# Seven buffers for x by features, its rows behind the weights on one queue, and the value passes' last sum formed later

## The chip, the cores and the metric

The kernel runs on one core of a Trainium2 chip. The metric is the device time of one execution in microseconds; the kernel before has a median of 1997.19 us over three runs (1996.58 to 2002.1). Its five engines run side by side and meet at semaphores: PE (TensorE, matmuls; PEld is its weight load), DVE (VectorE), ACT (ScalarE), POOL (GpSimd) and SP, which here only issues transfers. DMAs are issued from SP's queue, a few from POOL's and ACT's.

## The reference

One decoder layer and a final norm over x of 512 tokens by 2048 features in float32 (names as in the reference, cut):

```
h = rmsnorm(x, ln_mix)                                # x: (512, 2048)
proj = h @ w_in                                       # w_in: (2048, 4608)
sb_q, sb_k, sb_v, sw_q, sw_k, sw_v = split(proj)      # 1024 1024 1024 | 1024 256 256
sb_o = stick_breaking_attention(sb_q, sb_k, sb_v)     # 16 heads of 64, causal
sw_o = sliding_window_sink_attention(sw_q, sw_k, sw_v, sinks, slopes)   # 16 heads, 4 kv heads
x = x + concat(rmsnorm(sb_o), rmsnorm(sw_o)) @ w_out
x = x + (silu(h2 @ w_gate) * (h2 @ w_up)) @ w_down    # h2 = rmsnorm(x, ln_ffn), width 5632
return rmsnorm(x, ln_final)
```

The change touches only the first part: half of `sw_q` (512 columns of `w_in`), then `sb_v` (1024 columns), and the sum of squares of x for the first norm.

## The kernel before

Every float32 operand of a matmul is split in two rounded parts, hi and lo, and a product is three matmuls (hi hi, lo hi, hi lo). ACT writes hi as a rounded copy, DVE writes lo as the difference. x comes in twice: by features (`x_cols`, tiles `xt` of 128 features by 512 tokens, from `load_cols`, usually two features' tiles in one transfer) and by rows (`xr`, 128 tokens by 2048, from `load_rows`). From each feature tile kt, 0 to 15, `h_make` makes `hhi` (ACT, line 255) and `hlo` (DVE, line 256) scaled by the norm's gain `gcol`; the row factor of the norm is applied after the products. The rows serve only `x_squares`: four ACT squares per row tile into `ss1`.

**The projection of the queries, `add_kq`.** The work is eight slabs of 256 rows of `w_in`, W0 to W7, 512 columns each. A slab is a transfer into `raw` (ring of three), a split into `whi` (ACT, line 203) and `wlo` (DVE, line 204; rings of two), and 24 matmuls of 512 columns into four banks, named m and o (lines 548 to 550). `split` of slab s+1 is called from `step` in the third of slab s's eight groups, and `load` of the next two. `prep` makes the feature tiles that a later slab needs (the list `KTS`), and a step after it runs `flush` (the sums waiting in `vsum`) and the squares of one row tile. Slab 0 is split in two halves (the `L117` rows on `raw`, 128x512).

**The value passes.** `sb_v` is formed in two passes g = 0 and 1 over 1024 features each, as a 2x2 block product with seven products instead of eight (order `PD`: 1, 7, 6, 4, 5, 2, 3), each in two halves: 28 slots, in `value_slot` and the loop after it. The left factors of products 5, 7, 6 and 3 are sums of blocks of x times gain: with a the first 256 tokens and b the last 256, unprimed for the pass's first four feature tiles and primed for its last four,

- s1 = b + b' (product 5), s3 = a - b (product 7), s2 = b' - s3 (product 6) and s4 = a' - s2 (product 3), written by `left_sums` in steps of 128x256 into tiles `vs`.

In the kernel before, POOL begins s1 from the rounded parts (`hhi` + `hlo`, half columns), and the flushes on DVE do the rest: one step per tile for the first four tiles of a pass (s3), three for the last four (s1, s2, s4). `form` splits a sum into `vf` (hi on ACT, lo on POOL). The right factors are weight differences that POOL forms (`difference`: `t` and in place in `raw`, 128x1024), split by ACT (`hp`, a hi in PSUM for DVE to subtract, and `whi`) and DVE (`wlo`). `take` adds a product's banks to the accumulators `vacc` and `vu` on DVE.

**What sets the order.** A scheduler orders each engine's instructions, except those that are kept in program order (`dma` on SP and the calls through `pV`, `pA`, `pG`, `pT`, all listed at line 117). An engine works its list strictly in order and so does a queue: an entry that waits holds all behind it. On SP's queue stand `xt`, all weights and the value weights; the row tiles are issued on POOL's queue. A buffer's next load waits for the last reader of what it held: a new `xt` for the flush that reads the old one, a new `raw` for its whi and wlo. The last part of the setup (calls at the end of `add_kq`'s part, from `add_kq()` to `load_rows`) writes out by hand in which order these loads are issued.

Of the kernel before, what the change touches and what calls it, by code (L numbers as in the profile page):

```python
# [37 lines left out]
def tile_hymba(ctx: ExitStack, tc: tile.TileContext, x, x_cols, gains, w_in, sinks, w_out, w_gu, w_dn, ln_fin, out):  # L38
# [96 lines left out]
    def constants():  # L135
        V.tensor_scalar(out=neg1, in0=ones, scalar1=-1.0, scalar2=None, op0=ALU.mult)
        scr = tmp(F32, "scr")[:, 0:P]
        G.affine_select(out=scr, in_=ones, pattern=[[-1, P]], compare_op=ALU.is_ge, fill=0.0,
                        base=0, channel_multiplier=1)
        V.tensor_scalar(out=negu, in0=scr, scalar1=-1.0, scalar2=None, op0=ALU.mult)  # L140
        scs = tmp(F32, "scs")[:, 0:P]
        G.affine_select(out=scs, in_=ones, pattern=[[-1, P]], compare_op=ALU.is_gt, fill=0.0,
# [20 lines left out]
    def load(i):  # L163
# [133 lines left out]
    def load_cols(kt, n):  # L297
        xt = phase[1].tile([P, n, 512], F32, tag="xt", name="xt", bufs=5)
        dma(out=xt, in_=x_cols[kt * P:(kt + n) * P, :].rearrange("(a p) s -> p a s", p=P))
        for k in range(n):  # L300
            xs[kt + k] = xt[:, k, :]

    def load_rows(t):
        xr.append(phase[1].tile([P, D], F32, tag="xr", name="xr", bufs=4))
        pG.dma_start(out=xr[t], in_=x2d[t * P:(t + 1) * P, :])

# [10 lines left out]
    def left_sums(kt, xt):  # L317
        g, j, gc = kt // 8, kt % 4, gcol[:, kt:kt + 1]
        if kt % 8 == 0:
            vs = [v8.tile([P, 4, 512], F32, tag="v8", name="vs") for _ in range(2)]  # L320
            for k, p in enumerate("5736"):
                vleft[g, p] = vs[k // 2][:, :, (k % 2) * 256:(k % 2) * 256 + 256]
        s1, s3, s4, s2 = (vleft[g, p][:, j, :] for p in "5736")
        a, b = xt[:, 0:256], xt[:, 256:512]
# [4 lines left out]
        if kt % 8 < 4:  # L329
            pG.tensor_tensor(out=s1, in0=f(h_hi[kt])[:, 256:512], in1=f(h_lo[kt])[:, 256:512], op=ALU.add)  # L330
            vsum.append(lambda: stt(s3, a, s1, ALU.subtract))
        else:
            vsum.append(lambda: (stt(s1, b, s1, ALU.add), stt(s2, b, s3, ALU.subtract), stt(s4, a, s2, ALU.subtract)))

# [242 lines left out]
    class ValuePass(Block):  # L577
# [38 lines left out]
        def form(self, p, part):  # L616
# [4 lines left out]
            else:  # L621
                hl = vfm[self.g, p]
                pG.tensor_tensor(out=hl[:, :, 256:512], in0=src, in1=f(hl)[:, :, 0:256], op=ALU.subtract)

    vp = [ValuePass(g) for g in range(2)]
    for g in range(2):
# [4 lines left out]
        for k, fn, *args in ((-4, u.sum, "7", 0), (-3, u.sum, "5", 0), (-2, u.form, "7", "l"), (-1, u.sum, "6", 0),  # L631
                             (0, u.sum, "7", 1), (1, u.sum, "5", 1), (2, u.form, "6", "l"), (3, u.sum, "6", 1),
                             (4, u.sum, "4", 0), (5, u.sum, "4", 1), (6, u.form, "5", "l"), (8, u.form, "3", "l")):
            at_slot(b0 + k, "sum", fn, *args)
        for k, p in ((-4, "7"), (0, "6"), (4, "5"), (7, "3")):
            at_slot(b0 + k, "late", u.form, p, "h")
        for k, p in enumerate(PD):
            at_slot(b0 + 2 * k + 2, "take", u.take, p)
# [1214 lines left out]
```

## Time and profile before

| what | us |
|---|---|
| median of three runs | 1997.19 (1996.58 to 2002.1) |
| the profiled execution, its own time | 1999.97 |
| its span, first to last instruction | 1998.2 |
| PE busy | 1971.4 |
| DVE, ACT busy | 1496.2, 1497.5 |
| POOL busy | 1005.0 |
| mean granted TensorE clock | 0.995 of full speed |

All numbers of the trace come from this one execution. Times in its rows count from the span's start. A timeline row gives start, length, engine, line, operation, output and input tiles (numbers left out) with partitions x elements, a count if instructions follow each other, and in brackets how long the engine sat idle before it and what ended that. A matmul's listed length is longer than the distance to the next, since matmuls are pipelined; the distance is what counts. A stage row gives the stage, its length, busy time (and count) of PE, PEld, DVE, ACT and POOL, the granted clock, the DMA engines' busy share and GB/s.

### The profile page before, as it was taken

What the parts mean: (1) busy time and instruction counts of PE and PEld (TensorE: products, weight loads), DVE (VectorE), ACT (ScalarE), POOL (GpSimd) and SP (SyncE); (2) the same over time, 40 slices, a digit from 0 to 9 for tenths busy, and PEclk for the clock granted to TensorE, in tenths of its full rate; (3) what the DMA queues carried; (4) which work ended last, traced back from release to release, by engine and by line L of the source; (5) the groups of instructions that cost most, each with busy time, mean ns of one, the idle gap of its engine ahead of it and who ended that gap; (6) DMA issues with size and microseconds to landing.
All of it is one profiled execution on the core that took longest, in us unless ns stands there. A gap on an engine that the chain in (4) does not pass through costs nothing.

```text
span 1998.2 us, 28817 instructions
## 1 busy us (share of the span) xinstructions
PE 1971.4 (99%) x10132; PEld 1677.1 (84%) x10132; DVE 1496.2 (75%) x2051; ACT 1497.5 (75%) x2007; POOL 1005.0 (50%) x445
## 2 busy tenths in 40 slices
PE   8899999999999999999999999999999999999998
PEld 6688888898888888888888888888888888888886
DVE  7666888888974787777777777777777867767767
ACT  6675878877762487777777777777777788788787
POOL 3660000000010067576666757666675778878883
PEclk9999999999999999999999999999999999999999
DMA  8224543522333445445344454535444734433423
GB/s 304 86 75 113 140 123 100 147 74 64 112 114 133 148 122 132 132 106 143 104 135 118 120 133 106 143 101 137 116 122 113 277 143 132 163 127 114 176 80 116
DMA packets 290912, 256.99 MB, mean 129 GB/s; under 512 B 12544, under 2 KB 233744, under 8 KB 287824
## 3 DMA queue, kind: packets, MB, share of 16 engines
q1 hardware_dynamic: 288384, 244.10, 41.4%
q0 software_dynamic: 1952, 9.71, 1.3%
q8 instruction: 80, 1.31, 0.3%
q10 hardware_dynamic: 432, 1.34, 0.2%
q14 instruction: 64, 0.52, 0.1%
HBM read 222.59 MB, written 19.92 MB: 121 GB/s over the span
## 4 chain that ended last, share of the span: by engine, by line
PE 94%; DVE 2%; ACT 2%; DMA 1%; issue 1%; SPq 0%; DVEq 0%; ACTq 0%
PE o L117 36%; PE m L117 30%; PE m L397 3%; PE m L398 3%; PE m L399 3%; PE m L361 2%; PE m L363 2%; PE m L362 2%; PE o L361 1%; PE o L363 1%; PE o L362 1%; PE z L911 1%; PE z L117 1%; PE o L939 1%; DVE vs L117 1%; DMA raw<-in_w_in_dram 1%
## 5 line engine op out<-in xcount | busy, mean ns | idle before, releaser
L117 DVE TENSOR_TENSOR wlo<-t,hp 128x1024 fp32r<-128x1024 f32 x247 | 301.1, 1219 | 184.6 <-PE o L117 114.0
L117 POOL TENSOR_TENSOR t<-raw,t 128x1024 f32<-128x1024 f32 x111 | 282.5, 2545 | 281.1 <-ACT hp L117 269.1
L117 ACT ACTIVATE whi<-t 128x1024 fp32r<-128x1024 f32 x247 | 262.1, 1061 | 127.4 <-PE o L117 77.3
L117 PE MATMUL o<-hca,whi 128*128 128x512 f32 x880 | 307.5, 394 | 0.0
L117 POOL TENSOR_TENSOR t<-raw,raw 128x1024 f32<-128x1024 f32 x114 | 295.1, 2592 | 24.6 <-issue 11.5
L117 DVE TENSOR_TENSOR wlo<-raw,hp 128x1024 fp32r<-128x1024 f32 x187 | 228.3, 1221 | 91.7 <-issue 52.1
L117 ACT ACTIVATE whi<-raw 128x1024 fp32r<-128x1024 f32 (+1 forms) x189 | 199.8, 1057 | 105.6 <-PE m L117 75.2
L117 ACT ACTIVATE hp<-t 128x1024 fp32r<-128x1024 f32 x247 | 249.2, 1009 | 1.9 <-POOL t L117 1.8
L117 PE MATMUL o<-hca,wlo 128*128 128x256 f32 x880 | 241.4, 277 | 0.0
L117 PEld LDWEIGHTS o<-hca,whi 128*128 128x128 f32 x880 | 164.7, 188 | 38.0
L117 ACT ACTIVATE hp<-raw 128x1024 fp32r<-128x1024 f32 x191 | 192.8, 1010 | 3.3 <-DMA raw<-in_w_down_dram 2.2
L117 PE MATMUL m<-hca,whi 128*128 128x512 f32 x528 | 186.1, 394 | 1.1 <-DVE hca L117 1.1
L117 PEld LDWEIGHTS o<-hca,wlo 128*128 128x128 f32 x880 | 164.5, 188 | 0.4
L204 DVE TENSOR_TENSOR wlo<-raw,whi 128x1024 fp32r<-128x1024 f32 x87 | 111.5, 1282 | 54.0 <-ACT whi L203 52.2
L203 ACT ACTIVATE whi<-raw 128x1024 fp32r<-128x1024 f32 x87 | 91.9, 1056 | 79.1 <-PE o L363 38.3
L709 POOL TENSOR_TENSOR sqA<-sqA,oc 128x512 f32<-128x512 f32 x7 | 10.0, 1432 | 274.5 <-ACT oc L708 274.5
L117 PE MATMUL m<-whi,dca 128*128 128x512 f32 x592 | 146.9, 389 | 0.0
L117 PE MATMUL o<-whi,dca 128*128 128x512 f32 x592 | 146.8, 389 | 0.0
L117 PE MATMUL m<-hca,wlo 128*128 128x256 f32 x528 | 144.8, 277 | 0.0
L117 PEld LDWEIGHTS o<-whi,dca 128*128 128x128 f32 x592 | 111.1, 188 | 23.1
L117 PEld LDWEIGHTS m<-whi,dca 128*128 128x128 f32 x592 | 111.1, 188 | 23.0
L117 PE MATMUL m<-hcs,whi 128*128 128x512 f32 x352 | 126.6, 394 | 0.0
(360 smaller groups left out, 5191.5 us busy)
## 6 DMA issues: line engine op xcount, KB each, us to landing
raw<-in_w_gate_up_dram SPq DMA_DIRECT2D x348, 256.0 KB, 5.1
raw<-in_w_down_dram SPq DMA_DIRECT2D x68, 512.0 KB, 5.2
raw<-in_w_in_dram SPq DMA_DIRECT2D x35, 512.0 KB, 4.6
raw<-in_w_in_dram SPq DMA_DIRECT2D x66, 256.0 KB, 3.5
raw<-in_w_out_dram SPq DMA_DIRECT2D x32, 512.0 KB, 3.7
aT<-w SPq DMA_DIRECT2D x44, 256.0 KB, 3.4
xd<-aT SPq DMA_DIRECT2D x10, 1024.0 KB, 6.8
rx<-in_w_down_dram SPq DMA_DIRECT2D x20, 512.0 KB, 5.7
```

What stands on the lines that cost most here:

```text
L117: return lambda *a, **k: tc.keep_in_program_order(fn(*a, **k))
L203: A.activation(out=hi, in_=raw, func=AF.Copy)
L204: V.tensor_tensor(out=lo, in0=raw, in1=f(hi), op=ALU.subtract)
L361: mm(o, lhsT=lh[:, sl], rhs=hi[:, j, :], start=first, stop=False, skip_group_check=halves)
L362: mm(o, lhsT=lh[:, sl], rhs=lo[:, j, :], start=False, stop=False, skip_group_check=halves)
L363: mm(o, lhsT=ll[:, sl], rhs=hi[:, j, :], start=False, stop=(k == nslab * a - 1), skip_group_check=halves)
L397: mm(o, lhsT=wh, rhs=xh, start=(k == 0), stop=False)
L398: mm(o, lhsT=wh, rhs=xl, start=False, stop=False)
L399: mm(o, lhsT=wl, rhs=xh, start=False, stop=(k == KT - 1))
L709: G.tensor_tensor(out=acc, in0=acc, in1=t, op=ALU.add)
L911: mm(zb[:, o:o + r.shape[1]], lhsT=lhsT, rhs=r, start=False, stop=last, skip_group_check=True)
L939: mm(H.ob[:, c0:S], lhsT=vb, rhs=r[:, o:o + S - c0], start=(k == 3 and r is B.h), stop=(k == 0 and r is B.l), skip_group_check=True)
```

## The change

Five edits, all before the attention.

1. `xt` has seven buffers instead of five, and `xr` three instead of four. The temporaries `scr` and `scs` of `constants` now lie in `maskf`.
2. The loads: within slab 0 each feature tile is issued ahead of its half of W0; after W2 come all remaining feature tiles, then W3 and row tile 0, W4 and row tile 1, W5 and 2, W6 and 3, all on SP's queue. Row tiles leave POOL's queue.
3. s1 is begun by ACT (`pA`, a scaled copy of b) instead of by POOL.
4. s4 leaves the flushes. `last_sum` forms it in two DVE steps of 128x1024 in slots 6 and 7 of each pass: the hi part of a' minus s2, then plus the lo part. Product 3's `form` moves back one slot.
5. `constants` is called in slot 14 instead of after eight steps.

```
-            pG.tensor_tensor(out=s1, in0=f(h_hi[kt])[:, 256:512], in1=f(h_lo[kt])[:, 256:512], op=ALU.add)
+            pA.activation(out=s1, in_=b, func=AF.Copy, scale=gc)
             vsum.append(lambda: stt(s3, a, s1, ALU.subtract))
         else:
-            vsum.append(lambda: (stt(s1, b, s1, ALU.add), stt(s2, b, s3, ALU.subtract), stt(s4, a, s2, ALU.subtract)))
+            vsum.append(lambda: (stt(s1, b, s1, ALU.add), stt(s2, b, s3, ALU.subtract)))
...
+        def last_sum(self, half):
+            s4 = vleft[self.g, "3"]
+            h = f(h8s[2 * self.g + 1][half])[:, :, 0:256]
+            if half:
+                pV.tensor_tensor(out=s4, in0=s4, in1=h, op=ALU.add)
+            else:
+                pV.tensor_tensor(out=s4, in0=h, in1=vleft[self.g, "6"], op=ALU.subtract)
...
-        for k, p in ((-4, "7"), (0, "6"), (4, "5"), (7, "3")):
+        for k, p in ((-4, "7"), (0, "6"), (4, "5"), (8, "3")):
             at_slot(b0 + k, "late", u.form, p, "h")
+        for k in range(2):
+            at_slot(b0 + 6 + k, "late", u.last_sum, k)
...
-        pG.dma_start(out=xr[t], in_=x2d[t * P:(t + 1) * P, :])
+        dma(out=xr[t], in_=x2d[t * P:(t + 1) * P, :])
...
-    load_cols(6, 2)
-    defer(8, constants)
-    for c in range(4, 8):
-        while pos[0] < c - 4 or pos[1] < 3:
+    for c in range(3, 8):
+        load_cols(2 * c, 2)
+    for c in range(4):
+        while pos[0] < c or pos[1] < 3:
             step()
-        load_cols(2 * c, 2)
-        load_rows(c - 4)
+        load(c + 3)
+        load_rows(c)
```

Past the value passes every engine's instructions stand in the same order as before. SP's queue at the start, before: one feature transfer (`xt`) and one slab's weights (`raw`) in turn after W2.

```order
L99 DMA xt<-in_x_cols_dram 128x2x512
L99 DMA raw<-in_w_in_dram 128x2x512
L99 DMA xt<-in_x_cols_dram 128x2x512 x2
L99 DMA raw<-in_w_in_dram 128x2x512
L99 DMA xt<-in_x_cols_dram 128x2x512
L99 DMA raw<-in_w_in_dram 128x2x512
L99 DMA xt<-in_x_cols_dram 128x2x512
L99 DMA raw<-in_w_in_dram 128x2x512
L99 DMA xt<-in_x_cols_dram 128x2x512
L99 DMA raw<-in_w_in_dram 128x2x512 x3
```

The rows are feature tiles 4 and 5, W2, 6 to 9, W3, 10 and 11, W4 and so on. The same place now, up to the first weights of the value pass (the second of the last two `raw`):

```order
L99 DMA xt<-in_x_cols_dram 128x2x512
L99 DMA raw<-in_w_in_dram 128x2x512
L99 DMA xt<-in_x_cols_dram 128x2x512 x5
L99 DMA raw<-in_w_in_dram 128x2x512
L99 DMA xr<-in_x_dram 128x2048
L99 DMA raw<-in_w_in_dram 128x2x512
L99 DMA xr<-in_x_dram 128x2048
L99 DMA raw<-in_w_in_dram 128x2x512
L99 DMA xr<-in_x_dram 128x2048
L99 DMA raw<-in_w_in_dram 128x2x512
L99 DMA xr<-in_x_dram 128x2048
L99 DMA raw<-in_w_in_dram 128x2x512 x2
```

All feature tiles stand ahead of W3 and the four row tiles between W3 and W7. ACT's list, which the first products wait for, from slab 1's whi to slab 4's, before:

```order
L203 ACTIVATE whi<-raw 128x1024
L255 ACTIVATE hhi<-xt,gcol 128x512 x2
L203 ACTIVATE whi<-raw 128x1024
L255 ACTIVATE hhi<-xt,gcol 128x512 x4
L203 ACTIVATE whi<-raw 128x1024
L117 ACTIVATE xr,ss_110<-xr 128x512 x4
L255 ACTIVATE hhi<-xt,gcol 128x512 x2
L203 ACTIVATE whi<-raw 128x1024
```

And now up to the first squares, with the sums begun on ACT (`vs`):

```order
L203 ACTIVATE whi<-raw 128x1024
L255 ACTIVATE hhi<-xt,gcol 128x512 x2
L203 ACTIVATE whi<-raw 128x1024
L255 ACTIVATE hhi<-xt,gcol 128x512 x4
L117 ACTIVATE vs<-xt,gcol 128x256 x2
L255 ACTIVATE hhi<-xt,gcol 128x512
L117 ACTIVATE vs<-xt,gcol 128x256
L255 ACTIVATE hhi<-xt,gcol 128x512
L117 ACTIVATE vs<-xt,gcol 128x256
L255 ACTIVATE hhi<-xt,gcol 128x512 x4
L203 ACTIVATE whi<-raw 128x1024
L117 ACTIVATE xr,ss_110<-xr 128x512 x4
```

Ten feature tiles and four sums stand ahead of W3's whi where four feature tiles stood. DVE's list from the last flush on, before, with `wlo` of W7 (line 204), the copies of the projection's banks (`kq`) and the first value weights:

```order
L204 TENSOR_TENSOR wlo<-raw,whi 128x1024
L117 SCALAR_TENSOR_TENSOR vs<-xt,gcol,vs 128x256 x6
L204 TENSOR_TENSOR wlo<-raw,whi 128x1024
L557 COPY kq<-m 128x512
L117 TENSOR_TENSOR wlo<-rx,hp 128x1024
L557 COPY kq<-o 128x512
```

And now, from the same place to the two steps of `last_sum` in the first pass (`vs<-hhi,vs` and `vs<-vs,hlo`):

```order
L204 TENSOR_TENSOR wlo<-raw,whi 128x1024
L117 SCALAR_TENSOR_TENSOR vs<-xt,gcol,vs 128x256 x4
L204 TENSOR_TENSOR wlo<-raw,whi 128x1024
L557 COPY kq<-m 128x512
L557 COPY kq<-o 128x512
...
L117 COPY vu<-m 128x512 x2
L117 TENSOR_TENSOR vs<-hhi,vs 128x4x256
L117 TENSOR_TENSOR wlo<-raw_415,hp 128x1024
L117 TENSOR_TENSOR vs<-vs,hlo 128x4x256
L117 TENSOR_TENSOR wlo<-raw_455,hp 128x1024
L117 COPY vacc<-o 128x512 x2
```

The last flush has four steps instead of six, and two steps on whole tiles stand between the value pass's copies and weight splits.

More of the change, by code (lines that the diff above doesn't have):

```diff
@@ L136, in constants @@
         V.tensor_scalar(out=neg1, in0=ones, scalar1=-1.0, scalar2=None, op0=ALU.mult)
-        scr = tmp(F32, "scr")[:, 0:P]
+        scr, scs = maskf[:, 0:P], maskf[:, P:2 * P]
         G.affine_select(out=scr, in_=ones, pattern=[[-1, P]], compare_op=ALU.is_ge, fill=0.0,
@@ L140, in constants @@
         V.tensor_scalar(out=negu, in0=scr, scalar1=-1.0, scalar2=None, op0=ALU.mult)
-        scs = tmp(F32, "scs")[:, 0:P]
         G.affine_select(out=scs, in_=ones, pattern=[[-1, P]], compare_op=ALU.is_gt, fill=0.0,
@@ L180, in load @@
             for j in range(a):
+                load_cols(j, 1)
                 dma(out=raw[:, j, :], in_=srcs[0][j * P:(j + 1) * P, :])
@@ L297, in load_cols @@
     def load_cols(kt, n):
-        xt = phase[1].tile([P, n, 512], F32, tag="xt", name="xt", bufs=5)
+        xt = phase[1].tile([P, n, 512], F32, tag="xt", name="xt", bufs=7)
         dma(out=xt, in_=x_cols[kt * P:(kt + n) * P, :].rearrange("(a p) s -> p a s", p=P))
@@ L303, in load_rows @@
     def load_rows(t):
-        xr.append(phase[1].tile([P, D], F32, tag="xr", name="xr", bufs=4))
-        pG.dma_start(out=xr[t], in_=x2d[t * P:(t + 1) * P, :])
+        xr.append(phase[1].tile([P, D], F32, tag="xr", name="xr", bufs=3))
+        dma(out=xr[t], in_=x2d[t * P:(t + 1) * P, :])
     def h_make(kt):
@@ L322, in left_sums @@
                 vleft[g, p] = vs[k // 2][:, :, (k % 2) * 256:(k % 2) * 256 + 256]
-        s1, s3, s4, s2 = (vleft[g, p][:, j, :] for p in "5736")
+        s1, s3, s2 = (vleft[g, p][:, j, :] for p in "576")
         a, b = xt[:, 0:256], xt[:, 256:512]
@@ L632, in tile_hymba @@
                              (0, u.sum, "7", 1), (1, u.sum, "5", 1), (2, u.form, "6", "l"), (3, u.sum, "6", 1),
-                             (4, u.sum, "4", 0), (5, u.sum, "4", 1), (6, u.form, "5", "l"), (8, u.form, "3", "l")):
+                             (4, u.sum, "4", 0), (5, u.sum, "4", 1), (6, u.form, "5", "l"), (9, u.form, "3", "l")):
             at_slot(b0 + k, "sum", fn, *args)
-        for k, p in ((-4, "7"), (0, "6"), (4, "5"), (7, "3")):
+        for k, p in ((-4, "7"), (0, "6"), (4, "5"), (8, "3")):
             at_slot(b0 + k, "late", u.form, p, "h")
+        for k in range(2):
+            at_slot(b0 + 6 + k, "late", u.last_sum, k)
         for k, p in enumerate(PD):
@@ L655, in tile_hymba @@
     add_kq()
-    load_cols(0, 1)
     load(0)
-    load_cols(1, 1)
     load_cols(2, 2)
@@ L768, in tile_hymba @@
             split(8)
+        if n == 14:
+            constants()
         vof(n, "product")
```

## The prediction

> **What bounds the kernel now.** I read the page, then busy time by stages, then TensorE's timeline where a stage has a hole, then what each hole waited for.
>
> ```profile
> PE 1971.4 (99%) x10132; PEld 1677.1 (84%) x10132; DVE 1496.2 (75%) x2051; ACT 1497.5 (75%) x2007; POOL 1005.0 (50%) x445
> ...
> 5.35:23.72 18.37, 17.49 (x75) 13.23 (x73) 14.01 (x24) 7.38 (x10) 8.55 (x13) 1.00 0.84 314
> 23.72:28.46 4.74, 0.16 (x1) 0.00 (x1) 0.02 (x1) 2.44 (x4) 0.00 (x0) 1.00 1.02 397
> 28.46:36.36 7.90, 7.38 (x19) 5.50 (x19) 7.90 (x12) 7.90 (x21) 2.97 (x3) 0.57 0.81 296
> ...
> 54.70:62.96 8.26, 0.00 (x1) 0.00 (x1) 8.17 (x3) 0.00 (x0) 7.04 (x3) 0.81 0.25 69
> 62.96:69.80 6.84, 6.84 (x23) 5.49 (x23) 2.51 (x3) 2.46 (x3) 0.00 (x0) 0.73 0.45 149
> 69.80:150.00 80.20, 80.20 (x355) 66.44 (x354) 53.32 (x64) 61.56 (x65) 51.82 (x26) 1.00 0.23 73
> 150.00:1990.00 1840.00, 1836.89 (x9567) 1567.44 (x9566) 1388.36 (x1916) 1399.47 (x1874) 923.71 (x388) 1.00 0.43 126
> ```
>
> The first number after a stage's length is PE busy; the last three are granted clock, DMA share, GB/s. From 69.80 to 1990 PE is busy 1917.1 of 1920.2 us: nothing there is to be had by feeding it better. Before 69.80, where the key and query projection runs, it sits idle twice and twice runs at a reduced clock.
>
> ```profile
> 5.35 0.48 PE L548 MATMUL m<-hhi,whi 128*128 128x512 f32 x1
> ...
> 13.60 0.72 PE L550 MATMUL m<-hhi,wlo 128*128 128x512 f32 x2 [0.77 <-DVE wlo L204]
> ...
> 18.28 0.39 PE L548 MATMUL m<-hhi,whi 128*128 128x512 f32 x1
> ...
> 23.49 0.39 PE L550 MATMUL o<-hhi,wlo 128*128 128x512 f32 x1
> 28.46 0.50 PE L548 MATMUL m<-hhi,whi 128*128 128x512 f32 x1 [4.58 <-ACT whi L203]
> ...
> 62.96 0.79 PE L550 MATMUL m<-hhi,wlo 128*128 128x512 f32 x1 [8.29 <-DVE wlo L204]
> ...
> 69.80 1.07 PE L117 MATMUL m<-whi,hhi 128*128 128x512 f32 x4
> ```
>
> 18.28 and 23.49 are the first and last of slab 2's 24 matmuls, 23 steps apart: 0.2265 us each, 5.44 a slab. Eight slabs need 43.5 us; from 5.35 to 69.80 they take 64.45. So 20.95 us is lost: 2.06 in slabs 0 to 2 (18.37 - 72 x 0.2265), 4.74 and 8.3 idle, about 3.4 and 1.85 to the clock (0.43 of 7.90, 0.27 of 6.84), and 0.6 in short waits. That is the ceiling.
>
> The first hole waits for slab 3's weights (W3). The queue's timeline, the chain, and two stages of the DMA:
>
> ```profile
> 4.81 10.05 SPq L99 DMA_DIRECT2D xt<-in_x_cols_dram  x2
> 14.96 0.41 SPq L99 DMA_DIRECT2D raw<-in_w_in_dram  x1
> ...
> 14.96 12.29 DMA raw<-in_w_in_dram
> ...
> 4.00:12.50 8.50, 8.38 (x37) 6.40 (x36) 5.10 (x9) 6.11 (x9) 4.84 (x8) 1.00 0.95 355
> 16.00:32.00 16.00, 10.89 (x42) 8.31 (x41) 9.62 (x17) 5.98 (x14) 0.97 (x2) 0.91 1.01 393
> ```
>
> The sixth transfer of x by features (xt) has no buffer until 14.9, W3 stands behind it, and it then shares a full DMA with x by rows (xr) from POOL's queue: 12.29 us to land. The second hole waits for wlo of W7:
>
> ```profile
> 46.56 13.07 DVE L117 SCALAR_TENSOR_TENSOR vs<-xt,gcol,vs 128x256 f32<-128x256 f32 x6
> 59.55 3.35 DVE L204 TENSOR_TENSOR wlo<-raw,whi 128x1024 fp32r<-128x1024 f32 x1
> ...
> 49.37 2.48 POOL L117 TENSOR_TENSOR raw<-raw,rx 128x1024 f32<-128x1024 f32 x1
> ...
> 59.42 2.40 POOL L117 TENSOR_TENSOR raw<-raw,rx 128x1024 f32<-128x1024 f32 x1
> ...
> 15.81 1.40 DVE L256 SCALAR_TENSOR_TENSOR hlo<-xt,gcol,hhi 128x512 fp32r<-128x512 f32 x2
> 17.14 1.21 DVE L204 TENSOR_TENSOR wlo<-raw,whi 128x1024 fp32r<-128x1024 f32 x1
> 18.27 0.87 DVE L117 SCALAR_TENSOR_TENSOR vs<-xt,gcol,vs 128x256 f32<-128x256 f32 x2
> ```
>
> Two vs take 0.87 us alone and six 13.07 beside POOL's weight differences, one per POOL instruction: DVE gets in only between them. wlo of W7 stands behind these six.
>
> **The change part by part.** Wn are the eight slabs' weights; each xt is 0.52 MB (the first two half), each W 0.52, each xr 1.05.
>
> *Seven xt buffers, W3 behind all xt.* The first xt to need an old buffer is now 12-13, at the first vs flush, not 8-9. What the step needs from ACT, in its timeline and groups:
>
> ```profile
> 8.53 1.34 ACT L255 ACTIVATE hhi<-xt,gcol 128x512 fp32r<-128x512 f32 x2
> 9.88 1.06 ACT L203 ACTIVATE whi<-raw 128x1024 fp32r<-128x1024 f32 x1
> ...
> 13.85 1.34 ACT L255 ACTIVATE hhi<-xt,gcol 128x512 fp32r<-128x512 f32 x2 [0.15 <-DMA xt<-in_x_cols_dram]
> ...
> 67.26 0.60 ACT L555 ACTIVATE kq<-m 128x512 f32<-128x512 f32 x1 [15.74 <-PE m L550]
> ...
> L117 ACT ACTIVATE xr<-xr 128x512 f32<-128x512 f32 x16 | 9.8, 614 | 0.0
> ```
>
> xt 0-7 and W0-W2, 3.67 MB, had landed by 13.8 (the row at 13.85 waits for the last of them). In the new order 2.62 MB more carry xt 8-15 and W3: at 393 to 355 GB/s W3 lands at 20.5 to 21.2 instead of 27.25, if the queue never runs dry: xt 8-11 (1.05 MB) keep it fed 2.7 us past 13.8, and the flush frees a buffer at about 12.9 (below). Each pair xr, W after it takes 4.0 to 4.4: W4 lands at 25, W5 29, W6 33, W7 37 to 39. Their slabs start at 29.0, 34.5, 39.9, 45.3 (below), less 2.3 for the split (1.06 on ACT, 1.21 on DVE): they are in time, and none of the 4.74 idle is left but what the next step adds.
>
> *First sum on ACT.* Eight 128x256 activations go onto ACT, four ahead of whi of W1, four among the hhi ahead of whi of W3. The trace has none; 128x512 costs 0.614 and 128x1024 1.06, so 256 columns cost 0.22 and I take 0.614 - 0.22 = 0.39, between 0.2 and 0.614. The first stands ahead of slab 0's whi: PE starts 0.4 later, at 5.75. By ACT's order whi of W1 ends at 11.2 (before 10.94) and wlo of W1 at 12.4, ahead of its first use; slab 1 starts at about 11.5, where 5.35 + 5.44 = 10.8 would be without loss. So the 0.77 wait goes and 0.7 of the 2.06 stays; slab 2 ends at 11.5 + 10.9 = 22.4. From 13.8 ACT has ten hhi (half of 1.34 each) and four sums, 8.3: whi of W3 starts at 22.1 and ends at 23.2, slab 3 waits 0.8. DVE, after wlo of W1, has four vs (0.39, what the second adds in the row at 18.27), two hlo (0.66), wlo of W2 until 16.5, four vs and nine hlo, 7.5, and wlo of W3 until 25.2, wanted after slab 3's seventh matmul at 24.8: 0.4. I take 1.2 in all, between 0 and 2.5 (sums at 0.614, DVE steps at half of 1.40 and 0.87). The wait of 0.77 left the clock of its stage at 1.00, so I charge none to these, and the 3.4 goes.
>
> *Row transfers on SP.* Four issues leave POOL's queue for SP's, each ahead of a W; behind xr3, which waits for the first squares, stand W7 and the value weights. The squares (four of 0.614 per slab) stand on ACT ahead of each whi from W4 on. xr0 lands at 23.4, its squares end at 25.9, xr3 lands at 36 to 38. ACT needs 2.5 + 1.06 of a slab's 5.44 and hides them: cost 0. Without that slack a late xr would go to PE one for one.
>
> *The flushes lose the last sum.* Eight 128x256 steps go from DVE, eight sums from POOL. The last flush (four vs, 1.6) runs behind wlo of W6, whose buffer slab 4 frees at 34.5: 34.5 + 1.06 + 1.21 = 36.7 to 38.3. POOL's first difference reads a tile that lands two transfers behind W7, 39 to 42. So the flush is past, and only wlo of W7 (from 41) can meet POOL: 2.5 and 1.2, done by 45, wanted at 45.8. All 10.1 of the second hole and its clock goes; between 0 and the second rival's price.
>
> *End of the projection.* 11.5 + 7 x 5.44 + 1.2 = 50.8 against 69.80. ACT now has the kq copy ahead of the first hp: 0.60 + 1.06 + 1.06 fill the 2.7 us after the matmuls it waits for. I charge 0.3, up to 1: 51.1.
>
> *The last sum in the value pass.* Two 128x1024 DVE steps on SBUF per pass, 1.21 each by the row at 17.14; the value pass on DVE and POOL:
>
> ```profile
> 87.53 1.28 DVE L117 COPY vu<-m 128x512 f32<-128x512 f32 x2
> 89.11 1.22 DVE L117 TENSOR_TENSOR wlo<-raw,hp 128x1024 fp32r<-128x1024 f32 x1 [0.30 <-PE o L117]
> 91.83 1.22 DVE L117 TENSOR_TENSOR wlo<-raw,hp 128x1024 fp32r<-128x1024 f32 x1 [1.50 <-PE o L117]
> ...
> 84.68 2.41 POOL L117 TENSOR_TENSOR vf<-vs,vf 128x1024 fp32r<-128x1024 f32 x1
> 91.22 2.40 POOL L117 TENSOR_TENSOR vf<-vs,vf 128x1024 fp32r<-128x1024 f32 x1 [4.13 <-ACT vf L117]
> ...
> 126.97 2.41 POOL L117 TENSOR_TENSOR vacc<-vacc,vu 128x1024 f32<-128x1024 f32 x1 [1.80 <-DVE vu L117]
> ```
>
> They stand behind the vu copies (88.8), one on each side of a wlo. DVE has 1.5 + 0.3 idle per two products, and a wlo is wanted 4.5 us after its buffer is free (20 matmuls), so 2.4 fits. In the first pass POOL is idle from 87.1 until the vf that now waits for this sum; in the second the accumulation at 126.97 starts at the same moment: one wait of 2.4, some 0.5 on PE. I take 0.5 in all, between 0 and the rival's 4.7.
>
> *The constants* are called later, but their instructions stand in the same place on DVE and POOL: 0.
>
> Sum: 0.7 + 1.2 + 0.3 + 0.5 = 2.7 stays, and 0.25 for short waits: 20.95 - 2.95 = 18.0. The profiled execution took 1999.97 (span 1998.2) and would take 1982.0; it lies 2.8 above the median of 1997.19, so the median goes to 1979.2.
>
> **The rivals.** *The first hole stays* (0.14): whi and wlo of W3 now stand behind all hhi and hlo, and behind xt 12-15, which wait for a flush. If that chain is 4 us late, PE idles as at 23.72 and the clock falls again: 4.7 + 3.4 stay, gain 11, 1986. For: ACT and DVE are full there; against: margins worked out above. The Trainium skill (TensorE: Matmul & The Clock Gate, "What's actually happening") says that about 3.4 us idle halves the clock and as much work restores it. By that the slow stretch would cost 1.7; here it lasted 7.9 us at 0.57.
>
> *The second hole stays* (0.07): POOL's weights come before the flush. Then four vs at 2.5 end at 46.7 and wlo of W7 at 50.4, wanted at 45.8: 4.6 and the clock's 3.4 stay, gain 10, 1987. Against: the tile is issued after vs that stand before it, and lands behind W7.
>
> *DVE is locked in the value passes* (0.07): each of the four steps, and DVE behind it, waits for a whole POOL instruction as at 46.56. Two such steps (2.4 + 1.2) and two wlo end 9.6 us after the products' start, wanted at 7.25 (32 matmuls): 2.35 on PE per pass, 4.7 in both, 4.2 more than charged: 1983. POOL's idle time from 87.1 speaks against. The Trainium skill (SBUF — State Buffer, "Who interferes with whom") states this lock: a VectorE instruction with two SBUF inputs and a GpSimd one that reads SBUF exclude each other for a whole instruction. The row at 46.56 agrees, and so does the wlo at 91.83, whose second input lies in PSUM: it takes its 1.22 beside POOL's vf at 91.22.
>
> *One queue is slower than two* (0.04): if xr and W on SP went one at a time, by the page's
>
> ```profile
> raw<-in_w_in_dram SPq DMA_DIRECT2D x35, 512.0 KB, 4.6
> ...
> xr<-in_x_dram POOLq DMA_DIRECT2D x4, 1024.0 KB, 8.0
> ```
>
> each pair would take 12.6, W7 land at 20.6 + 50.4 = 71, the projection end at 79: 9 later than now, 2006. It decides once W7 lands after 62, under 207 GB/s. Against: 355 GB/s from SP alone at 4.00.
>
> *Nothing measurable* (0.05): losses only move; 1997.
>
> **How the numbers follow.** My forecast has 0.63. With the rivals that stay faster, faster by over 0.3% (6 us, about what a measurement of this kernel can tell) has 0.91, the same 0.05, slower 0.04. The range: low 1975.0, all 20.95 gone and 1.2 for the spread of the runs; high 1987.0, which takes in the unknown costs, the lock and the first rival.
>
> **What would show it.** Right: no PE gap over 2 us between 5.7 and 52; W3 landing near 21; value products from about 51; the last flush under 2 us; clock 1.00 throughout. Wrong: a stage at 0.5 clock, W7 landing after 44, vs in the value passes over 2 us each with PE waiting for wlo.

## The result, and the profile after

The changed kernel takes 1984.44 us (median of four runs, 1983.54 to 1986.93) where the kernel before took 1997.51 in the same comparison (four runs, 1996.58 to 2002.1): ratio 0.9932, 95% interval 0.9914 to 0.995. That is 13.1 us between the medians, 0.68% by the ratio. The forecast was 1979.2 within 1975.0 to 1987.0, so the sign and the range were right and the gain of 18 was 5 too large.

The profiled execution took 1986.93, the slowest of its four. First the page's engine row, then stages of it (columns as before: stage, length, busy us and count of PE, PEld, DVE, ACT, POOL, granted clock, DMA share, GB/s):

```profile
PE 1970.0 (99%) x10132; PEld 1681.1 (85%) x10132; DVE 1484.3 (75%) x2047; ACT 1501.0 (76%) x2015; POOL 994.0 (50%) x433
```

```profile
5.00:6.00 1.00, 0.56 (x4) 0.33 (x4) 0.84 (x2) 1.00 (x3) 0.00 (x0) 1.00 0.60 96
6.00:7.00 1.00, 1.00 (x6) 0.82 (x5) 1.00 (x2) 0.61 (x2) 0.00 (x0) 1.00 0.53 117
...
12.00:14.40 2.40, 2.40 (x8) 1.81 (x7) 1.82 (x5) 2.40 (x5) 0.68 (x2) 0.50 1.05 387
14.40:54.06 39.66, 38.98 (x171) 31.75 (x170) 27.53 (x46) 28.31 (x59) 12.18 (x6) 1.00 0.88 339
54.06:150.00 95.94, 95.91 (x426) 79.10 (x426) 70.21 (x84) 72.22 (x82) 55.75 (x28) 1.00 0.25 78
...
800.00:1400.00 600.00, 600.00 (x3446) 527.30 (x3445) 434.76 (x493) 474.27 (x524) 387.13 (x154) 1.00 0.46 122
```

Behind 14.40 PE is as good as never idle: both holes are gone. But there is a stage at half clock that was not forecast (12.00 to 14.40), and ahead of it two microseconds in which the DMA moved 96 and 117 GB/s. The kernel before in the same microseconds, and in the long stretch:

```profile
5.00:6.00 1.00, 1.00 (x7) 0.86 (x6) 1.00 (x2) 0.19 (x1) 0.46 (x1) 1.00 0.99 354
6.00:7.00 1.00, 1.00 (x6) 0.75 (x5) 0.06 (x1) 0.00 (x0) 0.66 (x1) 1.00 1.00 365
...
800.00:1400.00 600.00, 600.00 (x3456) 524.41 (x3455) 435.21 (x493) 474.96 (x525) 389.23 (x155) 1.00 0.46 123
```

PE's timeline of the changed kernel, where it waits and at the first value product:

```profile
5.65 0.50 PE L548 MATMUL m<-hhi,whi 128*128 128x512 f32 x1 [0.44 <-ACT whi L117]
...
8.28 0.39 PE L550 MATMUL o<-hhi,wlo 128*128 128x512 f32 x1
10.26 0.50 PE L548 MATMUL m<-hhi,whi 128*128 128x512 f32 x1 [1.59 <-ACT whi L117]
...
28.29 0.73 PE L550 MATMUL m<-hhi,wlo 128*128 128x512 f32 x2 [0.68 <-DVE wlo L204]
...
54.06 1.20 PE L117 MATMUL m<-whi,hhi 128*128 128x512 f32 x4
```

The wait at 10.26, in the middle of slab 0, is new. ACT's row says what it is: the second half of W0 arrives late. And POOL's rows show what else was issued early, the transfer of the attention's `sink` constant, and that the last flush on DVE now ends ahead of POOL's first weight difference:

```profile
9.57 0.63 ACT L117 ACTIVATE whi<-raw 128x512 fp32r<-128x512 f32 x1 [2.96 <-DMA raw<-in_w_in_dram]
```

```profile
2.00 0.72 POOL L148 DMA_DIRECT2D sink<-in_swa_sinks_dram  x1
...
41.84 2.40 POOL L117 TENSOR_TENSOR t<-raw,raw 128x1024 f32<-128x1024 f32 x1 [27.40 <-DMA rx<-in_w_in_dram]
```

```profile
39.92 1.67 DVE L117 SCALAR_TENSOR_TENSOR vs<-xt,gcol,vs 128x256 f32<-128x256 f32 x4
...
73.14 1.21 DVE L117 TENSOR_TENSOR vs<-hhi,vs 128x1024 f32<-128x1024 f32 x1
...
75.39 1.22 DVE L117 TENSOR_TENSOR vs<-vs,hlo 128x1024 f32<-128x1024 f32 x1
...
111.22 1.22 DVE L117 TENSOR_TENSOR vs<-hhi,vs 128x1024 f32<-128x1024 f32 x1
...
113.48 2.31 DVE L117 TENSOR_TENSOR vs<-vs,hlo 128x1024 f32<-128x1024 f32 x1
```

The flush ends at 41.59, a quarter of a microsecond ahead of 41.84. That order is not chance. With seven `xt` buffers the tile `t`, which POOL's first difference writes, lies where the last feature transfer lay; the last reader of that is the last step of the flush, and the program has POOL wait for it. In the kernel before `t` lies where a row tile lay, and POOL waits for transfers alone. Three of the four steps of `last_sum` take the 1.21 that was charged; the one that meets POOL takes 2.31.

Where the 13.04 of the two profiled executions (1999.97 and 1986.93) come from: the first value product is 15.74 earlier (69.80, now 54.06); from there to the end it took 2.54 more (1928.40, now 1930.94), though PE has 0.03 idle in the 95.94 us after it; and the time outside the span grew by 0.16. So two things had to be explained: the late start, and a long stretch that is slower with PE busy all the time (3446 matmuls between 800 and 1400 us instead of 3456).

### The profile page after: what moved, and what is told of

Its sections match the earlier page's. It is cut to its first block, busy times and chain, and to the rows that moved or that the text cites. A ratio compares the mean times of both kernels' runs of the same rounds, so it can differ in the third digit from the quotient of the medians.

```text
span 1985.0 us, 28804 instructions
## 1 busy us (share of the span) xinstructions
PE 1970.0 (99%) x10132; PEld 1681.1 (85%) x10132; DVE 1484.3 (75%) x2047; ACT 1501.0 (76%) x2015; POOL 994.0 (50%) x433
## 4 chain that ended last, share of the span: by engine, by line
PE 95%; ACT 2%; DVE 1%; DMA 0%; issue 0%; SPq 0%; DVEq 0%; ACTq 0%
PE o L117 36%; PE m L117 30%; PE m L397 3%; PE m L398 3%; PE m L399 3%; PE m L361 2%; PE m L363 2%; PE m L362 2%; PE o L361 1%; PE o L363 1%; PE o L362 1%; PE z L921 1%; PE z L117 1%; PE o L949 1%; PE z L1120 1%; PE z L874 1%
```

## The experiments

Every kernel was compared with the kernel before on the same chip. The first column of times is the first value product in its profile, which sums up the part that the change touches. Where two variants are compared below, their medians are. The four from "the same again" to "last sum only" share one chip, the next four a second, the next three a third; as 3456 and 3445 matmuls come on the first of these, and 3456 and 3408 on the second, that count does not go by the chip.

| kernel | first value product | matmuls 800 to 1400 | median us (runs) | ratio to before, 95% interval |
|---|---|---|---|---|
| before (first profile) | 69.80 | 3456 | 1997.51 (1996.58 to 2002.1) | |
| changed kernel | 54.06 | 3446 | 1984.44 (1983.54 to 1986.93) | 0.9932 [0.9914, 0.995] |
| the same again | 53.99 | 3456 | 1984.23 (1983.67 to 1984.49) | 0.9933 [0.9916, 0.9951] |
| late sink | 51.27 | 3456 | 1981.07 (1980.82 to 1981.54) | 0.9918 [0.9901, 0.9935] |
| loads only | 53.24 | 3445 | 1984.48 (1983.7 to 1986.27) | 0.9936 [0.9915, 0.9958] |
| last sum only | 60.52 | 3456 | 1989.29 (1988.47 to 1991.38) | 0.9964 [0.9949, 0.9979] |
| late sink, first sum on POOL | 52.01 | 3457 | 1982.59 (1982.37 to 1982.82) | 0.9917 [0.9902, 0.9931] |
| late sink, s4 in the flushes | 50.59 | 3457 | 1981.13 (1980.94 to 1981.36) | 0.9909 [0.9894, 0.9924] |
| late sink, W3 ahead | 49.99 | 3456 | 1980.24 (1979.93 to 1980.78) | 0.9905 [0.9888, 0.9923] |
| POOL gated | 59.06 | 3408 | 2001.25 (2000.47 to 2001.68) | 1.0013 [1.0003, 1.0022] |
| POOL gated in place | 59.02 | 3445 | 1991.4 (1989.45 to 1992.59) | 0.9984 [0.9968, 1.0001] |
| W3 ahead, 128 bytes on | 49.75 | 3409 | 1991.06 (1990.58 to 1991.46) | 0.9978 [0.9961, 0.9996] |
| W3 ahead, 96 bytes on | 50.03 | 3425 | 1987.14 (1986.45 to 1987.37) | 0.9954 [0.9938, 0.9969] |
| before again | 70.17 | 3456 | 2000.62 (one run) | |

**The changed kernel again.** No edit.

> The changed kernel unaltered, to see whether its late start repeats. In its first profile the second half of W0 landed near 9.5 us, PE waited 1.59 us for it, and PE ran at a reduced clock to 14.4. Theory A (the sink's transfer, issued on POOL's queue at 2.00 us, holds up SP's transfers): the same again, DMA under 150 GB/s between 5 and 7 us, a wait of 1.2 to 2.0 us in slab 0. Rival B (chance of that one execution): the half lands near 7, no wait, the first value product near 51. Time 1983.5 to 1987 by A, 1981 by B. The long stretch behind 54 us took 2.5 us more in that execution than before; if this is a property of the execution and not of the change, it may be gone here (first value product to the end 1928.4 instead of 1930.9).

The late start repeats, with 85 and 148 GB/s between 5 and 7 us; the slower stretch does not. Its rows at the same two places:

```profile
10.18 0.50 PE L548 MATMUL m<-hhi,whi 128*128 128x512 f32 x1 [1.67 <-ACT whi L117]
...
53.99 1.20 PE L117 MATMUL m<-whi,hhi 128*128 128x512 f32 x4
```

```profile
800.00:1400.00 600.00, 600.00 (x3456) 524.42 (x3455) 436.11 (x494) 475.69 (x525) 388.94 (x155) 1.00 0.46 123
```

With a span of 1982.4, 1928.41 us follow 53.99, the same as before's 1928.40. So the 2.54 belonged to that one execution, and the two `last_sum` steps per pass cost PE nothing.

**The sink's transfer late.** On the changed kernel:

```
-        nc.gpsimd.dma_start(out=sink, in_=sinks[0].partition_broadcast(P))
+        pG.dma_start(out=sink, in_=sinks[0].partition_broadcast(P))
```

> As the changed kernel, but the sink's transfer is kept behind POOL's last instruction that stands ahead of slot 14, so that it is issued after the queries' projection; nothing else moves but one DVE step of 128x128. Theory A (it holds up the first weights): W0's second half lands at 7.1 to 7.6, the wait of 1.59 goes and with it the reduced clock (about 1.6 more), first value product at 50.6 to 51.2 instead of 54.06, time 3.2 below the changed kernel's, 1981.2. Rival B (the new order of the queue, the feature tile ahead of the weight's second half, delays it): one tile of 0.26 MB, at 355 GB/s 0.74 us; W0's second half at 9 or later, time as the changed kernel's within 0.5. Rival C (sums on ACT delay the split): the landing is early, the wait stays above 1.

It is issued at 11.11 (not behind the projection, as the expectation said: the POOL instructions that it now stands behind end there). The stages and PE's waits:

```profile
5.00:6.00 1.00, 1.00 (x6) 0.88 (x6) 0.83 (x2) 1.00 (x3) 0.00 (x0) 1.00 0.96 305
6.00:7.00 1.00, 1.00 (x6) 0.80 (x5) 0.79 (x2) 0.40 (x2) 0.00 (x0) 1.00 0.99 367
```

```profile
11.51 0.50 PE L548 MATMUL m<-hhi,whi 128*128 128x512 f32 x1 [0.29 <-ACT whi L203]
...
25.50 0.73 PE L550 MATMUL m<-hhi,wlo 128*128 128x512 f32 x2 [0.87 <-DVE wlo L204]
...
51.27 1.19 PE L117 MATMUL m<-whi,hhi 128*128 128x512 f32 x4
```

The DMA is at 305 and 367 GB/s, W0's second half is in time, the wait and the half clock are gone, and the time is 3.16 lower than in the run before, 3.2 having been expected; the first value product, at 51.27, just misses the 50.6 to 51.2. Theory A is shown: one transfer of 8 KB on POOL's queue, issued at 2.00, cost 3.2 us. Why these few packets hold up the other queue for two microseconds there, and hardly at 11.11, is not shown; the time of issue alone does not decide it, as the run with the first sum on POOL shows below.

**The loads alone.** On the kernel before (each feature tile ahead of its half of W0 is in it too):

```
-                xt ... bufs=5    xr ... bufs=4, pG.dma_start
+                xt ... bufs=7    xr ... bufs=3, dma (SP's queue)
 ...
+    defer(8, constants)
+    for c in range(3, 8):
+        load_cols(2 * c, 2)
+    for c in range(4):
+        ...
+        load(c + 3)
+        load_rows(c)
```

> The kernel before with the edits on buffers and loads alone (seven xt, three xr, the rows on SP's queue, W3 behind all feature tiles); the first sum stays on POOL, s4 in the flushes, the constants deferred by eight steps, their temporaries of their own. Theory A (both holes come from the loads; the last flush is past before POOL's first weight difference at about 41): both holes go, six vs near 39 take under 3.5 us, first value product 51 to 53, time 1980 to 1984. By A the sink, now issued near 12, makes its dip there (under 150 GB/s for 2 us between 12 and 16) and W3 may be some 2 us late. Rival B (the second hole needs the shorter flush): the last vs run into POOL's differences, at least three of them at 2.2 us, PE waits 3 to 8 us for wlo of W7, time 1987 to 1992.

PE, the last flush (still six vs) and POOL's first difference:

```profile
25.91 0.73 PE L551 MATMUL m<-hhi,wlo 128*128 128x512 f32 x2 [1.87 <-DVE wlo L205]
32.69 0.73 PE L551 MATMUL m<-hhi,wlo 128*128 128x512 f32 x2 [1.04 <-DVE wlo L205]
53.24 1.19 PE L117 MATMUL m<-whi,hhi 128*128 128x512 f32 x4
```

```profile
39.11 2.71 DVE L117 SCALAR_TENSOR_TENSOR vs<-xt,gcol,vs 128x256 f32<-128x256 f32 x6
```

```profile
42.26 2.41 POOL L117 TENSOR_TENSOR t<-raw,raw 128x1024 f32<-128x1024 f32 x1 [12.90 <-DVE vs L117]
```

Both holes go with the loads alone, as by theory A, though product and time lie just above its 51 to 53 and 1980 to 1984. POOL's row shows the wait named above: it sat idle until the flush was over (41.82). The dip that theory A expected from the sink did not come: it was issued at 11.17, and the lowest of the microseconds from 11 to 17 has 303 GB/s. What is left is 2.9 us of waits for wlo of W3 and W4, on a DVE that has the longer flushes and POOL's first sums beside it.

**The last sum alone.** On the kernel before:

```
-            vsum.append(lambda: (stt(s1, b, s1, ALU.add), stt(s2, b, s3, ALU.subtract), stt(s4, a, s2, ALU.subtract)))
+            vsum.append(lambda: (stt(s1, b, s1, ALU.add), stt(s2, b, s3, ALU.subtract)))
...
+            at_slot(b0 + 6 + k, "late", u.last_sum, k)
```

> The kernel before with s4 alone taken out of the flushes and formed in slots 6 and 7 by two steps of 128x1024; loads and first sum as before. Theory A (each vs of the last flush that meets POOL costs one POOL instruction, 13.07 / 6 = 2.18): four instead of six, wlo of W7 4.4 us earlier, the hole of 8.29 becomes 3.9, with 0.5 for the steps in the value passes time 1992 to 1994; the first hole (4.58 for whi of W3) stays. Rival B (the flush is let through only when POOL pauses): the hole stays over 7, time 1996 to 1998. Rival C (the steps in the value passes cost what the flush gains): the hole shrinks, but PE waits over 2 us per pass for a wlo near the products 5 and 2, time 1997 or more.

```profile
29.96 0.79 PE L548 MATMUL m<-hhi,whi 128*128 128x512 f32 x1 [5.93 <-ACT whi L203]
60.52 1.07 PE L117 MATMUL m<-whi,hhi 128*128 128x512 f32 x4
```

```profile
46.55 1.66 DVE L117 SCALAR_TENSOR_TENSOR vs<-xt,gcol,vs 128x256 f32<-128x256 f32 x4
```

```profile
48.14 2.40 POOL L117 TENSOR_TENSOR t<-raw,raw 128x1024 f32<-128x1024 f32 x1 [7.64 <-DMA raw<-in_w_in_dram]
```

None of the three expectations held: the second hole is not halved but gone, and the kernel is 7.1 faster than the 1996.38 of before in this comparison (ratio 0.9964). The flush is not charged per vs. With the old loads POOL does not wait for it, and the two race: the four vs are done at 48.21 as POOL starts at 48.14, so nothing locks them. Two steps fewer in the last flush would not do that alone. It begins 1.59 ahead of POOL here, and 0.04 and 0.25 ahead in the two profiles of before, where four steps would have met POOL too. The earlier flushes are shorter as well. That the first hole is longer here (5.93 instead of 4.58) is not the reason: before's second profile has 6.02. The first hole stays, as expected.

**The first sum back on POOL, and s4 back in the flushes**, each on the late-sink kernel:

```
-            pA.activation(out=s1, in_=b, func=AF.Copy, scale=gc)
+            pG.tensor_tensor(out=s1, in0=f(h_hi[kt])[:, 256:512], in1=f(h_lo[kt])[:, 256:512], op=ALU.add)
```

> The kernel with the late sink (1981.07), with the first sum begun by POOL again as before; all else equal. Theory A (slab 3's wait of 0.87 is DVE's chain, not ACT's): ACT's eight sums of 0.40 go, so PE starts up to 0.2 earlier and the wait of 0.29 in slab 1 goes, but DVE meets eight POOL instructions of 0.73 to 1.1, and W3's wlo stands behind ten hlo instead of nine: a wait of 1 to 2 there, time 1981.0 to 1982.5. Rival B (ACT is what slab 3 waits for): 3.2 us less on ACT, no wait at W3, time 1979.5 to 1980.5. Rival C (POOL's sums hold DVE for whole instructions): waits of over 2, 1983 or more.

```
-            vsum.append(lambda: (..., stt(s2, b, s3, ALU.subtract)))
+            vsum.append(lambda: (..., stt(s2, b, s3, ALU.subtract), stt(s4, a, s2, ALU.subtract)))
...
-            at_slot(b0 + 6 + k, "late", u.last_sum, k)
```

> The kernel with the late sink (1981.07), with s4 back in the flushes and the two steps of 128x1024 out of the value passes; all else equal. Theory A (the last flush, now six vs of 0.39, still ends before POOL's first difference near 39 to 41, so the second hole does not come back; the eight steps are on DVE ahead of wlo of W3 and W4): waits of 1 to 2 us more for these two, as in the kernel with the loads alone, time 1982 to 1983.5. Rival B (the shorter flush is what removes the second hole): the last vs take over 5 us beside POOL, PE waits over 3 for wlo of W7, 1986 or more. Rival C (the steps in the value passes cost PE what they were charged, 0.5 or more, and the flushes have room): 1980.0 to 1980.8.

PE's longest wait in the first, then in the second with its last flush and POOL's first difference:

```profile
26.46 0.73 PE L550 MATMUL m<-hhi,wlo 128*128 128x512 f32 x2 [1.06 <-DVE wlo L204]
```

```profile
24.82 0.73 PE L550 MATMUL m<-hhi,wlo 128*128 128x512 f32 x2 [1.02 <-DVE wlo L204]
```

```profile
36.49 2.71 DVE L117 SCALAR_TENSOR_TENSOR vs<-xt,gcol,vs 128x256 f32<-128x256 f32 x6
```

```profile
40.16 2.40 POOL L117 TENSOR_TENSOR t<-raw,raw 128x1024 f32<-128x1024 f32 x1 [29.15 <-DMA rx<-in_w_in_dram]
```

The first sum on ACT is worth 1.5 us (1982.59 against 1981.07, and against the 1981.13 of the other kernel on its own chip); theory A's upper end (1982.5) is just passed. Of this 0.74 lies ahead of the first value product, where PE's longest wait is for wlo behind ten hlo on DVE, as in theory A; where the rest lies is not shown. In this kernel the sink's transfer is issued at 13.08, and the DMA has the dip of the changed kernel once more, here between 15 and 17 us and with PE busy throughout:

```profile
15.00:16.00 1.00, 1.00 (x6) 0.82 (x5) 1.00 (x3) 1.00 (x3) 0.00 (x0) 1.00 0.58 73
16.00:17.00 1.00, 1.00 (x6) 0.82 (x5) 1.00 (x2) 1.00 (x2) 0.00 (x0) 1.00 0.91 93
```

So what made the dip dear in the changed kernel is that PE was waiting for the very weights that it held up. The last sum in the value pass is worth nothing once the loads are right: 1981.13 against 1981.07. The flush of six ends at 39.20, still ahead of 40.16, and as POOL waits for it with these loads, the second hole had no way back. Theory A expected 1 to 2 more and rival C a gain; neither came.

**W3 ahead of the last feature tiles**, on the late-sink kernel:

```
-    for c in range(3, 8):
+    for c in range(3, 6):
         load_cols(2 * c, 2)
+    load(3)
+    for c in range(6, 8):
+        load_cols(2 * c, 2)
```

> The kernel with the late sink (1981.07), with W3 issued ahead of feature tiles 12 to 15 instead of behind them. DVE then has five hlo ahead of W3's wlo instead of nine and the other five behind it. Theory A (the order of hlo and wlo on DVE is what slab 3 waits for): the wait of 0.87 goes, W4's wlo ends 1 to 2 us later, a wait of 0 to 0.5 in its place, time 1980.0 to 1981.0; no wait over 0.6 between 12 and 50 us. Rival B (DVE is full through slabs 3 and 4, the wait only moves): 0.7 to 1.5 at slab 4, time 1981 to 1982. It is also the try at a version faster than both kernels.

From just ahead of PE's first product (5.60) to the first value product:

```profile
5.40:49.99 44.59, 44.58 (x195) 36.03 (x193) 33.80 (x54) 33.63 (x68) 11.32 (x7) 1.00 0.98 366
```

Theory A: no wait is left, the eight slabs take 44.4 where 43.5 was the floor. 1980.24 is the best time here, 4.2 below the changed kernel.

**POOL held back in the kernel before.** One POOL instruction ahead of its first difference reads what the last flush writes:

```
+        last = sm.tile([P, 1], F32, tag="gate", name="gate")
+        pG.tensor_copy(out=last, in_=vleft[1, "3"][:, 3, 0:1])
...
```

> The kernel before, with one POOL instruction of 128x1 ahead of POOL's first weight difference, that reads what the last step of the last flush writes: so POOL's differences cannot start before the flush is over. All loads and all sums as before, six vs in the last flush. Theory A (the second hole is those vs being let in one by one between POOL's differences; in before's runs, 1989.3 to 2002.3, their number varies): the six vs take 2.4 to 3 us instead of 13.07, wlo of W7 is ready by 52, no wait of over 1 for it, the first hole stays, time 1988 to 1990.5 with runs within 3 us of each other. Rival B (the flush is slow of itself or for another reason, the DMA of 50 to 60 us say): the six take over 6 us, POOL now starts later, and the time is 1997 or more. Rival C (POOL's delay comes out one for one at the first value products): the hole for wlo goes, but PE waits 2 to 4 us near the first value product, 1991 to 1994.

```profile
47.13 2.71 DVE L117 SCALAR_TENSOR_TENSOR vs<-xt,gcol,vs 128x256 f32<-128x256 f32 x6
```

```profile
59.06 1.07 PE L117 MATMUL m<-whi,hhi 128*128 128x512 f32 x4
```

```profile
800.00:1400.00 600.00, 600.00 (x3408) 521.73 (x3407) 424.69 (x487) 468.79 (x518) 386.48 (x154) 1.00 0.45 120
```

Locally theory A holds to the letter: six vs in 2.71, no second hole, first value product 10.7 earlier. The gate does by hand what the new place of `t` does in the changed kernel. Yet the time is 2001.25. Only rival B's 1997 or more takes that in, and its sign, six vs over 6 us, did not come: the hidden layer runs 1.4% slower (3408 matmuls; the kernel before has 3456 in its profile, not the 3460 that the next expectation writes). The small tile had moved nearly all later tiles by 128 bytes in SBUF. Three runs separate the two. The first is the gate without a tile of its own; the others are the kernel with W3 ahead and an unused tile of 128 and of 96 bytes a partition:

```
-        last = sm.tile([P, 1], F32, tag="gate", name="gate")
-        pG.tensor_copy(out=last, in_=vleft[1, "3"][:, 3, 0:1])
+        last = vleft[1, "3"][:, 3, 0:1]
+        pG.tensor_copy(out=last, in_=last)
```

> The gated kernel again, with the POOL instruction of 128x1 copying one column of the flush's last tile onto itself instead of into a small tile of its own. That tile had moved nearly every later tile by 128 bytes in SBUF, and there the matmuls of the hidden layer ran at 3408 in 600 us (800 to 1400) instead of 3460, which ate the 10.7 us that the gate had gained up to the first value product (59.06 instead of 69.80). Theory A (the gate removes the second hole; the slower pace came with the addresses): 3449 to 3460 matmuls in that stretch, first value product 58 to 60, time 1987.5 to 1990.5. Rival B (the pace came with the later start of POOL's differences): 3408 again, time 2000 to 2002.

```
+    G.memset(const.tile([P, 32], F32, name="pad"), 0.0)
```

> The kernel with the late sink and W3 ahead of the last feature tiles (1980.24), with an unused constant of 128 bytes a partition that moves the later tiles by 128 bytes, as in the first gated kernel; the order of the work is the same. Theory A (the addresses set the pace of the hidden layer's matmuls): near 3408 matmuls between 800 and 1400 us instead of 3456, time 1991 to 1994. Rival B (the addresses do nothing): 3456, time 1980.0 to 1980.8.

```
+    G.memset(const.tile([P, 24], F32, name="pad"), 0.0)
```

> The same with an unused constant of 96 bytes, so that the activation and weight tiles begin at multiples of 256 bytes instead of 32 or 160 beyond one. If addresses set the pace, some other place than the present one may be faster: 3456 matmuls at 231.7 and 114.7 ns for a pair of 512 and 256 columns, where the queries' projection keeps 226.5 for 512, leave 2% at most. I expect a change of either sign, 1970 to 1994; 1980.0 to 1980.8 if addresses do nothing.

The stage of the gate in place, and of the two shifts:

```profile
800.00:1400.00 600.00, 600.00 (x3445) 527.33 (x3444) 434.17 (x493) 473.93 (x523) 389.40 (x154) 1.00 0.46 121
```

```profile
800.00:1400.00 600.00, 600.00 (x3409) 521.74 (x3408) 424.60 (x488) 469.26 (x518) 380.48 (x151) 1.00 0.45 121
```

```profile
800.00:1400.00 600.00, 600.00 (x3425) 524.24 (x3424) 428.39 (x488) 471.32 (x520) 383.47 (x153) 1.00 0.43 123
```

The addresses set the pace: 128 bytes cost 10.8 us with one MEMSET of the unused tile as the only other change, 96 bytes 6.9, and 3408 and 3409 come on two chips. With the addresses of the kernel before, the gated kernel takes 1991.4, 0.9 above the range of theory A, and its 3445 matmuls lie just under the 3449 to 3460; rival B's 3408 did not come back. Its interval against the kernel before still reaches 1.

**The kernel before again.** No edit.

> The kernel before unaltered, a second profile. Its 58 runs so far lie between 1988.72 and 2002.89, those of every other kernel within 3.2 of each other. Theory A (the second hole is a race between the last flush and POOL's first difference, and comes out differently from one execution to the next): time and first value product move together, so that the product stands at 69.80 less what this execution's time is below 1999.97, within 3 for the pace of the hidden layer; at 1990 it would stand near 60 and the last six vs take 2.7, at 1996 near 66 with some of the six held up, at 2001 again near 70. Rival B (the spread is the pace of the hidden layer): product within 1 of 69.80 whatever the time, and a count between 800 and 1400 us that differs from 3460 by over 20 if the time differs by over 4. If the time is within 2 of 1999.97 the run tells nothing new.

```profile
63.61 0.79 PE L550 MATMUL m<-hhi,wlo 128*128 128x512 f32 x1 [10.14 <-DVE wlo L204]
```

It took 2000.62 with the full second hole, so by its own terms it tells nothing new. That before's fastest executions (1988.72) lose less in that hole was argued, not shown.

## Why the prediction was right, and where it was off

**What held.** PE starts at 5.65 (5.75 forecast). No hole is left at W3 or W7. Slab 3 waits 0.68 for wlo alone (1.2 forecast); in the late-sink kernel 0.87. The sums on ACT follow each other at 0.40 (0.39). The row squares never hold up PE. The last flush ends at 41.59, and at 38.80 without the late start (36.7 to 38.3). Without the late start W3 lands at 20.6 (20.5 to 21.2) and the first value product stands at 51.27 (51.1). Neither the lock in the value passes nor a slow single queue came: one step of `last_sum` took over 2 us, but PE did not wait for it.

**Right with half the reason: the second hole.** The prediction had the flush past POOL's first difference by time, and against the rival that the tile which POOL reads is issued after vs that stand before it. What keeps the order in every kernel with the new loads is that POOL waits for the flush itself, which comes with the place of `t`. The prediction did not see that; this part was luck.

**The step that failed: the constants.** The prediction said that their instructions "stand in the same place on DVE and POOL: 0". On neither is that so. On DVE one of them moved up by one place. On POOL two first sums stood ahead of them before, which waited for hlo, the second of them until 8.77, and the transfer stood behind the MEMSET of `maskf`. POOL's rows before, from that sum to the transfer, and that MEMSET in the changed kernel:

```profile
8.77 1.12 POOL L117 TENSOR_TENSOR vs<-hhi,hlo 128x256 f32<-128x256 f32 x1 [2.12 <-DVE hlo L256]
...
12.09 0.30 POOL L146 MEMSET maskf<- 128x256 f32 x1
12.35 0.72 POOL L149 DMA_DIRECT2D sink<-in_swa_sinks_dram  x1
```

```profile
13.65 0.31 POOL L145 MEMSET maskf<- 128x256 f32 x1 [10.73 <-DVE negs L144]
```

The change took the sums off POOL, so that the constants start at 1.51; and the transfer, which is not kept in program order, now stands ahead of the MEMSETs, the larger of which waits for DVE since the temporaries lie in `maskf`. Together that let the transfer out at 2.00, into the first weights; kept behind the MEMSET it goes out at 11.11. The profile after charges 1.59 of wait and the rest to the clock and the later slabs; moving this transfer alone gave back 3.16. So a stage at half clock, which the prediction named as a sign of being wrong, did come, though not from a hole at W3 or W7.

**The term that failed: the distance to the median.** The sum gave 1982.0 for an execution like the profiled one, and 2.8 was then taken off because that execution lay 2.8 above before's median. But before's executions spread from 1988.72 to 2002.89, the other kernels' by 3.4 at most, and both profiles of before (1999.97 and 2000.62) show the hole in full. So the offset most likely lay in the hole, which the change removes, and not in the rest of the kernel. It is not shown: the profiled execution also lies above its own median in nine of the twelve profiles of the other kernels, by up to 2.49 (the changed kernel's first), so a part of the 2.8 may be of that kind. Without that step: 1982.0 + 3.16 for the sink - 0.5 for the last sum's charge = 1984.7, against 1984.44 measured. The late-sink kernel (1981.07) stands against 1981.5.

**A term charged too high.** The last sum was charged 0.5 and costs nothing: the one step that met POOL took 2.31 at 113.48, and DVE's slack covered it.

**What carried the gain.** The prediction gave the second hole's end to shorter flushes and earlier loads together. Either is enough: the loads alone bring 1984.48 (with the sink late of itself), the last sum alone 1989.29, and with the loads in place the last sum adds nothing. All five edits (1984.44) bring no more than the loads alone, because the early sink takes back 3.2. With the old loads the second hole is decided by who comes first, the flush or POOL's first difference; with the new ones POOL waits for the flush.

## What to carry to other kernels

When an instruction is taken off an engine, list what stood behind it in that engine's queue, transfers above all: they now start when it used to wait, and a small one can land in the middle of the loads that start the kernel. Where one engine's work ends just ahead of another's, look whether a wait put it there: an order by chance has to be kept by timing, one by a wait does not. The difference between a profiled execution and the median can belong to one stage; before adding it to a forecast, ask whether the change removes that stage. And compare kernels at the same tile addresses, or count matmuls in a stretch that the change doesn't touch, before calling an edit slow.

## What the runs showed of the hardware that was not expected

- The pace of matmuls depends on where their tiles lie. At three places 0, 96 and 128 bytes apart, 600 us of the hidden layer held 3456, 3425 and 3409 matmuls; over the program 0, 6.9 and 10.8 us. No place tried was faster than the present one.
- At the same addresses there are still two paces: 3456 and 3445 or 3446 (the changed kernel's two profiles had one each), about 2.5 us a run, the same in each of the three pieces of 200 us. What chooses is open.
- 8 KB on POOL's queue, issued at 2.00, brought the DMA from some 360 to 96 and 117 GB/s for two microseconds, and issued at 13.08 to 73 and 93. Issued at 11.11 its packets ran near 15 us, and 338 GB/s was the lowest of the microseconds around. What decides is open. The Trainium skill (DMA: Bandwidth & Descriptors, "Queues, rings and completion order") says that each DMA engine takes turns between queues packet by packet. By that sixteen small packets should cost next to nothing, as they did at 11.11; the other two cases show more.
- A wait of 1.59 us in slab 0 was followed by half clock until about 14.6 (0.50 in the stage from 12.00), one of 1.87 at 25.91 in the loads-only kernel was not:

```profile
25.90:28.00 2.10, 2.09 (x9) 1.75 (x10) 2.10 (x3) 1.78 (x5) 2.10 (x3) 1.00 1.08 423
```
